# Small products of the recurrent scan in block 1: two steps of the scan issued as one run, on four PSUM banks

## The chip, the cores and the metric

One core of a Trainium2 chip runs the whole program. The metric is device time in microseconds (us), the median of the runs. The engines are PE (TensorE), DVE (VectorE), ACT (ScalarE), POOL (GpSimd) and SP (SyncE, here the queue from which most transfers are issued).

## The reference

The program computes three blocks on 512 tokens of width 1024. The change lies in the first, in its recurrent branch: a gated linear recurrence over chunks of 32 tokens, with 8 heads of 128 x 128 state, run once forward and once backward over the sequence.

```python
HG_CHUNK = 32
def gla_chunk_scan(q, k, v, log_f):            # (B, T, H, 128)
    ...
    qc, kc, vc, gc = chunks(q), chunks(k), chunks(v), chunks(log_f)
    b = jnp.cumsum(gc, axis=3)
    b_last = b[:, :, :, -1, :]
    q_t = qc * jnp.exp(b)
    k_t = kc * jnp.exp(-b)
    k_s = kc * jnp.exp(b_last[:, :, :, None, :] - b)
    a = jnp.where(lower, jnp.einsum('nbhik,nbhjk->nbhij', q_t, k_t), 0.0)
    o_intra = jnp.einsum('nbhij,nbhjv->nbhiv', a, vc)
    def step(state, xs):
        q_n, k_n, v_n, dec_n = xs
        o_n = jnp.einsum('bhik,bhkv->bhiv', q_n, state)
        state = dec_n[..., None] * state + jnp.einsum('bhik,bhiv->bhkv', k_n, v_n)
        return state, o_n
    _, o_inter = lax.scan(step, s0, (q_t, k_s, vc, jnp.exp(b_last)))
    ...
o_fwd = hgrn2_scan(q_b, i_b, zf_fwd, lb_f)
o_bwd = jnp.flip(hgrn2_scan(jnp.flip(q_b, 1), jnp.flip(i_b, 1), jnp.flip(zf_bwd, 1), lb_b), 1)
```

## The kernel before, in words

The recurrent branch is the function `hgrn`. It takes the 8 heads in four pairs. For a pair, `project` makes the projections of the hidden state (queries, the two gates, values, the output gate) with large matrix products; the helper `mm` (L102 to L104) does each as three products of exact halves, so the rows L102, L103 and L104 are the projections. Then `scan` does the recurrence of the pair: `m` counts its two heads, `d` the two directions, and the 16 chunks of 32 tokens are 16 steps.

A step of `scan` has up to eight small products on PE and four vector operations on DVE:

- the o products (L527): queries of the chunk against the state before it. 32 columns of PE are used, and the result goes into 32 partitions of the bank `ob[m]`; `tile_position=(0, po)` says which strip of 32 columns, with po = 32 x (chunk mod 4).
- the u products (L535): keys of the chunk against its values, 32 rows of PE deep, `tile_position=(po, 0)`: a strip of 32 rows. Each step takes two PSUM banks for them, one for each direction, which holds both heads.
- the four operations on DVE (L547, or a copy L544 at the first step): new state = old state x decay + u. The o products of the next step read it.

A product in float32 shows as two instructions in the trace, so a step has 8 + 8 of them.

Order of the work: `scan` and `ends` (normalise, turn and gate the pair's outputs) are generators. While `project` of the next pair runs, a `Side` object advances them by one or two yields at each yield of `project`; what is left when `project` ends is drained (`side.drain()`), and for the last pair the eight gate projections after the loop (L594) do the same. That is the order in which the code is written. A scheduler (the tile framework's, by its own timeline) then orders the instructions of each engine: it takes what is ready by its reckoning, earlier code first. It therefore mixes small products of neighbouring steps, and puts them between projections.

All PSUM tiles of block 1 (`ps`, `o`, `u`) share one ring of eight banks. A scan holds two for `ob`; the projections use one after the other.

## Time and profile before

| | us |
|---|---|
| runs: median (lowest to highest of 3) | 3543.41 (3537.98 to 3550.98) |
| span of the profiled execution | 3547.4 |
| PE busy in it | 3200.2 (90%) |
| DVE busy | 1552.2 (44%) |
| ACT busy | 1013.6 (29%) |
| POOL busy | 971.3 (27%) |

The page gives the profiled execution's span and lists no time around it; the span lies 4.0 us above the median of the runs and inside their range. Busy shares are means over the whole program, whose parts differ. The small products of the scan run from 459 to 859 us of the span, and only that stretch bears on the change.

In a timeline a row is: start, length, engine, line, operation, output and inputs, count. Rows of one PE line that follow one another are merged, and a length includes the time in which a product passes through the array, so the difference of two starts, not the length, is what a product takes from PE.

### The profile page before, as it was taken

To read this page: it belongs to the slowest core of one execution; us is meant where nothing else is said; L and a number is where in the kernel's file an instruction comes from. 1 tells how busy PE (TensorE), PEld (TensorE's weight loads), DVE (VectorE), ACT (ScalarE), POOL (GpSimd) and SP (SyncE) were. 2 spreads that over 40 slices of the span, in tenths; PEclk is the share of its full clock that TensorE was granted. 3 is DMA by queue.
4 is the path that set the end of the run, shared out by engine and by line. 5 is a ranking of instruction groups with operands and counts; after the bars stand their busy time and mean duration, and the time that the engine had idled before them with its cause. 6 is when DMAs were issued, how large, how long until landed. Compare 5 with 4: busy or idle time off the path is not lost.

```text
span 3547.4 us, 52376 instructions
## 1 busy us (share of the span) xinstructions
PE 3200.2 (90%) x21072; PEld 2087.7 (59%) x21072; DVE 1552.2 (44%) x3435; ACT 1013.6 (29%) x2175; POOL 971.3 (27%) x859
## 2 busy tenths in 40 slices
PE   8999999999989889979999999799777578699988
PEld 6898777776766856663333333578656467433322
DVE  3324544423339678542233222531477877422222
ACT  4334323322221356311111111312365452110000
POOL 5343423232332454220000000433564444000000
PEclk9999999999989999879999999899887789899999
DMA  4121211113536433048988886253222133799998
GB/s 152 48 72 53 67 60 59 50 60 93 163 90 181 130 108 102 25 166 341 345 330 335 312 323 260 86 157 121 78 79 63 63 94 115 293 409 409 409 409 350
DMA packets 372551, 625.93 MB, mean 176 GB/s; under 512 B 43998, under 2 KB 240525, under 8 KB 372310
## 3 DMA queue, kind: packets, MB, share of 16 engines
q1 hardware_dynamic: 367190, 603.58, 47.9%
q0 software_dynamic: 5120, 19.01, 1.4%
q8 instruction: 166, 2.72, 0.3%
q14 instruction: 75, 0.61, 0.1%
HBM read 596.61 MB, written 25.91 MB: 175 GB/s over the span
## 4 chain that ended last, share of the span: by engine, by line
PE 73%; DVE 11%; DMA 8%; ACT 4%; issue 2%; POOL 2%; SPq 1%; POOLq 0%; ACTq 0%; DVEq 0%
PE ps L102 11%; PE h L1604 10%; PE ps L103 10%; PE ps L104 10%; PE yb L1643 7%; DMA w<-in_moe_w_dram 5%; PE hc L1604 3%; PE ps L1586 2%; PE o L527 2%; PE u L535 1%; PE ps L913 1%; PE ob L749 1%; DVE acc L1087 1%; PE ps L2240 1%; DMA aw<-in_ada_w_dram 1%
## 5 line engine op out<-in xcount | busy, mean ns | idle before, releaser
L201 POOL TENSOR_TENSOR wlo<-wraw,whi 128x1024 fp32r<-128x1024 f32 (+5 forms) x219 | 422.9, 1952 | 828.6 <-ACT whi L197 810.0
L1604 PE MATMUL h<-w,xT 128*64 128x512 f32 x2048 | 465.1, 601 | 22.4 <-DMA w<-in_moe_w_dram 16.9
L1604 PEld LDWEIGHTS h<-w,xT 128*64 128x64 f32 x2048 | 141.6, 137 | 335.9 <-issue 255.2
L1643 PE MATMUL yb<-w,hT 128*64 128x512 f32 (+1 forms) x1536 | 304.5, 604 | 17.8 <-ACT hT L1627 15.4
L197 ACT CAST whi<-wraw 128x2048 fp32r<-128x2048 f32 (+4 forms) x108 | 161.5, 1496 | 239.2 <-PE ps L103 128.0
L1464 POOL DMA_INDIRECT xs<-xh,ii x20 | 21.3, 1066 | 732.4 <-DVE sl L1467 712.0
L1643 PEld LDWEIGHTS yb<-w,hT 128*64 128x64 f32 (+1 forms) x1536 | 88.0, 129 | 200.6 <-issue 159.2
L1612 DVE SCALAR_TENSOR_TENSOR th<-th,h 128x512 f32<-128x512 f32 x32 | 22.0, 688 | 415.0 <-ACT th L1611 415.0
L102 PE MATMUL ps<-hT,whi 128*128 128x512 f32 x416 | 173.4, 417 | 0.0
L102 PE MATMUL ps<-whi,hT 128*128 128x512 f32 (+1 forms) x424 | 165.2, 390 | 4.0 <-DVE hT L316 4.0
L103 PE MATMUL ps<-hT,wlo 128*128 128x512 f32 x416 | 166.0, 399 | 0.0
L104 PE MATMUL ps<-hT,whi 128*128 128x512 f32 x416 | 165.9, 399 | 0.0
L1611 ACT ACTIVATE th<-h 128x512 f32<-128x512 f32 x32 | 19.1, 597 | 501.5 <-PE h L1604 501.5
L103 PE MATMUL ps<-whi,hT 128*128 128x512 f32 (+1 forms) x424 | 157.4, 371 | 0.0
L104 PE MATMUL ps<-wlo,hT 128*128 128x512 f32 (+1 forms) x424 | 154.5, 367 | 0.0
L115 POOL TENSOR_TENSOR rs<-rs_t,mhalf 128x8 f32<-128x8 f32 (+3 forms) x78 | 95.3, 1226 | 122.3 <-DVE rs_t L110 100.9
L1604 PE MATMUL hc<-w,xT 128*32 128x512 f32 x1024 | 124.2, 598 | 0.0
L1656 DVE TENSOR_TENSOR ys<-yb,g 64x512 f32<-64x512 f32 x64 | 44.1, 689 | 182.8 <-PE yb L1643 182.3
L547 DVE SCALAR_TENSOR_TENSOR s<-s,ec,u 128x128 f32<-128x128 f32 x224 | 65.3, 342 | 128.3 <-PE u L535 126.1
L102 PEld LDWEIGHTS ps<-whi,hT 128*128 128x128 f32 x424 | 104.4, 246 | 15.2 <-issue 4.9
L103 PEld LDWEIGHTS ps<-whi,hT 128*128 128x128 f32 x424 | 104.7, 247 | 7.8 <-issue 3.5
L1087 DVE SCALAR_TENSOR_TENSOR acc<-glu,w,acc 128x798 f32<-128x798 f32 x90 | 107.0, 1223 | 1.0
(810 smaller groups left out, 7031.3 us busy)
## 6 DMA issues: line engine op xcount, KB each, us to landing
w<-in_moe_w_dram SPq DMA_DIRECT2D x376, 1024.0 KB
wraw<-in_w_in_dram SPq DMA_DIRECT2D x48, 1024.0 KB
aw<-in_ada_w_dram SPq DMA_DIRECT2D x192, 256.0 KB
wraw<-in_od_w_in_dram SPq DMA_DIRECT2D x27, 512.0 KB
rows<-rw_rows SPq DMA_DIRECT2D x48, 192.0 KB
w<-in_moe_w_dram POOLq DMA_DIRECT2D x8, 1024.0 KB, 9.1
xh<-xn SPq DMA_DIRECT2D x10, 512.0 KB
wraw<-in_w_proj_b_dram SPq DMA_DIRECT2D x4, 1024.0 KB
```

What stands on the lines that cost most here:

```text
L102: nc.tensor.matmul(out, L[0], R[0], start=start, stop=False)
L103: nc.tensor.matmul(out, L[1], R[0], start=False, stop=False)
L104: nc.tensor.matmul(out, L[0], R[1], start=False, stop=stop)
L115: nc.gpsimd.tensor_tensor(out, t, mh.to_broadcast(list(ss.shape)), op=ALU.pow)
L197: nc.scalar.copy(hi, raw)
L201: eng.tensor_tensor(lo[:, a:b], raw[:, a:b], hi[:, a:b].bitcast(F32), op=ALU.subtract)
L527: nc.tensor.matmul(ob[m][po2:po2 + 32, t2 * 128:t2 * 128 + 128], X["qx", d][:, m, c2], tt[d, m], start=False, stop=(n == 15), skip_group_c ...
L547: nc.vector.scalar_tensor_tensor(s, tt[d, m], X["ec", d][:, m * 16 + cp:m * 16 + cp + 1], u, ALU.mult, ALU.add)
L1087: v.scalar_tensor_tensor(acc[:, c], glu[:, c, j:j + W], w2[:, j, c:c + 1], acc[:, c], ALU.mult, ALU.add)
L1586: nc.tensor.matmul(b, back, y[:, hs], start=(i == 0), stop=(i == len(terms) - 1))
L1604: nc.tensor.matmul(bb[o:o + cap], lhs, w[:, kk % 2, fh * 512:fh * 512 + 512], start=(kk == 0), stop=(kk == 7), tile_position=(0, o))
L1643: nc.tensor.matmul(yb[o:o + cap], lhs, w[:, j, dh * 512:dh * 512 + 512], start=first, stop=last, tile_position=(0, o))
```

## The change

Only `scan` is changed. The loop takes two steps at a time: first the o products of the last two steps, then the u products of the next two, for one head in both directions and both steps, then for the other head. The u products of two steps lie in four banks. Every small product gets an order-only edge (no semaphore) to the last DVE operation of the two steps before it, so the scheduler may not put it ahead of that one. State tiles have three buffers in place of two. There is one yield after each step's vector operations and one after each pair, so a scan now has 24 yields in this loop where it had 16.

```diff
-        tt = {}
-        for n in range(16):
-            if n > 0:
-                for m in range(2):
+        tt, ub, last, st = {}, {}, None, mybir.DependencyInfo(mybir.DependencyClass.NoSync, mybir.DependencyReason.DATA)
+        place = lambda d, n: (n // 4, 32 * (n % 4)) if d == 0 else ((15 - n) // 4, 32 * ((15 - n) % 4))
+
+        def together(mm):
+            if last is not None:
+                k.tc.add_manual_dep(mm.ins, last.ins.name, st, reason="together")
+        for n in range(0, 18, 2):
+            for m in range(2):
+                for i in (n - 2, n - 1):
                     for d in range(2):
-                        c2 = n if d == 0 else 15 - n
...
+                        if i > 0:
+                            c = i if d == 0 else 15 - i
+                            t, po = place(d, i)
+                            together(nc.tensor.matmul(ob[m][po:po + 32, t * 128:t * 128 + 128], X["qx", d][:, m, c], tt[d, m, i - 1],
+                                                      start=False, stop=(i == 15), skip_group_check=True, tile_position=(0, po)))
-            if n < 15:
-                ub = [bank("u"), bank("u")]
+            steps = [i for i in (n, n + 1) if i < 15]
+            for i in steps:
                 for d in range(2):
...
+                    ub[d, i] = bank("u")
+            for m in range(2):
+                for i in steps:
+                    for d in range(2):
+                        t, po = place(d, i)
+                        together(nc.tensor.matmul(ub[d, i][:, m * 128:m * 128 + 128],
+                                                  kt[d][po:po + 32, m, t], v[po:po + 32, t, m * 128:m * 128 + 128],
+                                                  start=True, stop=True, tile_position=(po, 0)))
+            for i in steps:
                 for d in range(2):
...
-                        s = T([128, 128], f"s{d}{m}", 2)
+                        s = T([128, 128], f"s{d}{m}", 3)
...
+                            last = nc.vector.scalar_tensor_tensor(s, tt[d, m, i - 1], X["ec", d][:, m * 16 + cp:m * 16 + cp + 1], u, ALU.mult, ALU.add)
+                        tt[d, m, i] = s
+                yield
             yield
```

What it does to the order of the instructions is seen at three places. In the rows, o is an output bank of a pair, u a bank of u products, s with two digits the state of direction and head, qx the queries, kt the keys, v the values; a number behind a name tells tiles apart.

PE, second pair of heads, one run between projections, as it was before:

```order
L104 MATMUL ps_4158<-hT1_91,whi_3939 128x512
L527 MATMUL o_4018<-s00_4132,qx0_3396 32x128
L535 MATMUL u_4175<-v_3593,kt0_3964 128x128
L527 MATMUL o_4019<-s01_4134,qx0_3396 32x128
L535 MATMUL u_4175<-v_3593,kt0_3964 128x128
L535 MATMUL u_4176<-v_3593,kt1_3992 128x128
L527 MATMUL o_4018<-s10_4136,qx1_3565 32x128
L527 MATMUL o_4019<-s11_4138,qx1_3565 32x128
L527 MATMUL o_4018<-s00_4150,qx0_3396 32x128
L527 MATMUL o_4019<-s01_4152,qx0_3396 32x128
L535 MATMUL u_4176<-v_3593,kt1_3992 128x128
```

PE, the same pair, a run of the changed kernel:

```order
L104 MATMUL ps_4444<-hT1_91,whi_4217 128x512
L536 MATMUL o_4018<-s00_4339,qx0_3380 32x128
L536 MATMUL o_4018<-s10_4343,qx1_3503 32x128
L536 MATMUL o_4018<-s00_4393,qx0_3380 32x128
L536 MATMUL o_4018<-s10_4397,qx1_3503 32x128
L536 MATMUL o_4019<-s01_4341,qx0_3380 32x128
L536 MATMUL o_4019<-s11_4345,qx1_3503 32x128
L536 MATMUL o_4019<-s01_4395,qx0_3380 32x128
L536 MATMUL o_4019<-s11_4399,qx1_3503 32x128
L546 MATMUL u_4465<-v_3541,kt0_3964 128x128
L546 MATMUL u_4466<-v_3541,kt1_3992 128x128
L546 MATMUL u_4467<-v_3541,kt0_3964 128x128
```

Before, o and u products alternate, and neighbours often share a strip; now eight o products stand together, four strips of 32 columns for each head, and then eight u products (five more rows follow) on four strips of 32 rows and four banks. Over the four pairs the small products stood in 80 runs with 142 changes between o and u inside them; now they stand in 31 runs with 33 changes.

PE, second pair, where the projections of the pair have ended and the rest of the scan is drained (new in the changed kernel; the same in the third pair):

```order
L546 MATMUL u_4517<-v_3541,kt0_3964 128x128
L546 MATMUL u_4518<-v_3541,kt1_3992 128x128
L536 MATMUL o_4018<-s00_4485,qx0_3380 32x128
L536 MATMUL o_4018<-s10_4489,qx1_3503 32x128
L536 MATMUL o_4018<-s00_4527,qx0_3380 32x128
L536 MATMUL o_4018<-s10_4531,qx1_3503 32x128
L536 MATMUL o_4019<-s01_4487,qx0_3380 32x128
L536 MATMUL o_4019<-s11_4491,qx1_3503 32x128
L536 MATMUL o_4019<-s01_4529,qx0_3380 32x128
L536 MATMUL o_4019<-s11_4533,qx1_3503 32x128
L546 MATMUL u_4551<-v_3541,kt0_3964 128x128
```

No projection stands between two runs here: three runs, 44 products, follow one another, where before no run had more than 12 products. Elsewhere between two runs of the changed kernel lie 12 to 48 projections.

PE at the end of the branch, before and then in the changed kernel (L568 and L581 turn the outputs of the last pair, oha is the first operand of the next stage):

```order
L103 MATMUL ps_6192<-hT0_90,wlo_6030 128x512
L104 MATMUL ps_6192<-hT1_91,whi_6029 128x512
L568 MATMUL ps_6218<-cc_58,kt0_6169 128x128 x4
L568 MATMUL ps_6225<-cc_58,kt0_6169 128x128 x4
L102 MATMUL ps_6302<-oha0_6237,whi_6147 128x512
```

```order
L546 MATMUL u_6186<-v_4979,kt1_5522 128x128
L536 MATMUL o_5556<-s00_6169,qx0_4822 32x128
L536 MATMUL o_5556<-s10_6173,qx1_4945 32x128
L536 MATMUL o_5557<-s01_6171,qx0_4822 32x128
L536 MATMUL o_5557<-s11_6175,qx1_4945 32x128
L536 MATMUL o_5556<-s00_6191,qx0_4822 32x128
L536 MATMUL o_5557<-s01_6193,qx0_4822 32x128
L536 MATMUL o_5556<-s10_6195,qx1_4945 32x128
L536 MATMUL o_5557<-s11_6197,qx1_4945 32x128
L581 MATMUL ps_6218<-cc_58,kt0_6208 128x128 x4
L581 MATMUL ps_6225<-cc_58,kt0_6208 128x128 x4
L102 MATMUL ps_6302<-oha0_6237,whi_6073 128x512
```

Before, 41 projections lie between the last o product and the first L568; now none. On POOL, the power of the last pair (ors, L115) stood ahead of the two operations of 1024 columns that split the next weights, and now stands behind them:

```order
L201 TENSOR_TENSOR wlo<-wraw,whi 128x512 x2
L201 TENSOR_TENSOR wlo<-wraw,whi 128x1024 x2
L115 TENSOR_TENSOR ors<-rs_t,mhalf 128x8
L201 TENSOR_TENSOR wlo<-wraw,whi 128x512 x2
```

That is the changed kernel; before, the second and third of these rows stood the other way round.

## Rows read from the trace of the kernel before

**Rows 1.** Page, part 1: busy time of each engine.
```profile
PE 3200.2 (90%) x21072; PEld 2087.7 (59%) x21072; DVE 1552.2 (44%) x3435; ACT 1013.6 (29%) x2175; POOL 971.3 (27%) x859
```

**Rows 2.** Windows, 459.2 to 859.2 us: length; busy us of PE, PEld, DVE, ACT, POOL; clock.
```profile
459.20:859.20 400.00, 396.82 (x2372) 301.69 (x2372) 148.62 (x330) 106.05 (x118) 116.14 (x52) 0.99 0.17 55
```

**Rows 3.** Chain of waits, 459 to 860 us, by line (its head).
```profile
by line: PE ps L102 20.0%; PE ps L103 17.9%; PE ps L104 17.7%; PE o L527 13.7%; PE u L535 12.9%; PE ps L511 2.7%; DVE gb L459 2.4%; issue 2.0%; DVE ga L451 1.8%; ACT ga L454 1.3%; PE ps L502 1.3%; DVE gb L457 1.1%; ACT whi L197 0.9%; PE o L
```

**Rows 4.** Groups by form, PE, 459.2 to 859.2 us: busy us, mean ns | idle before.
```profile
L527 PE MATMUL o<-s,qx 128*32 128x128 f32 x480 | 67.1, 283 | 3.2 <-DVE s L547 2.9
L535 PE MATMUL u<-v,kt 32*128 32x128 f32 x480 | 62.4, 305 | 0.0
```

**Rows 5.** Timeline, PE: four u products on two strips; eight on four.
```profile
458.92 0.40 PE L104 MATMUL ps<-hT,whi 128*128 128x512 f32 x1
459.25 0.72 PE L535 MATMUL u<-v,kt 32*128 32x128 f32 x8
459.90 0.50 PE L102 MATMUL ps<-hT,whi 128*128 128x512 f32 x1
...
570.47 0.39 PE L103 MATMUL ps<-hT,wlo 128*128 128x512 f32 x1
570.71 0.40 PE L104 MATMUL ps<-hT,whi 128*128 128x512 f32 x1
571.03 0.75 PE L535 MATMUL u<-v,kt 32*128 32x128 f32 x16
571.71 0.50 PE L102 MATMUL ps<-hT,whi 128*128 128x512 f32 x1
```

**Rows 6.** Timeline, PE: the chopped run shown in the order above.
```profile
574.39 0.40 PE L104 MATMUL ps<-hT,whi 128*128 128x512 f32 x1
574.90 0.41 PE L527 MATMUL o<-s,qx 128*32 128x128 f32 x2
...
578.37 0.50 PE L102 MATMUL ps<-hT,whi 128*128 128x512 f32 x1
```

**Rows 7.** Timeline, PE: four o products on two strips, then eight u products.
```profile
586.79 0.28 PE L103 MATMUL ps<-whi,hT 128*128 128x256 f32 x1
586.91 0.28 PE L104 MATMUL ps<-wlo,hT 128*128 128x256 f32 x1
587.12 0.63 PE L527 MATMUL o<-s,qx 128*32 128x128 f32 x8
587.68 0.75 PE L535 MATMUL u<-v,kt 32*128 32x128 f32 x16
588.35 0.39 PE L102 MATMUL ps<-whi,hT 128*128 128x256 f32 x1
```

**Rows 8.** Timeline, DVE: the state operations of two steps, back to back.
```profile
506.09 2.13 DVE L547 SCALAR_TENSOR_TENSOR s<-s,ec,u 128x128 f32<-128x128 f32 x8
```

**Rows 9.** Timeline, DVE, 587 to 597 us: operations of a direction's gate around states.
```profile
587.72 3.25 DVE L459 TENSOR_TENSOR_SCAN gb<-keep,ga 128x1024 f32<-128x1024 f32 x1 [1.12 <-ACT ga L454]
...
593.43 1.23 DVE L465 TENSOR_TENSOR qt<-q,eb 128x1024 f32<-128x1024 f32 x1 [1.19 <-ACT eb L460]
...
596.49 1.22 DVE L472 TENSOR_TENSOR qx<-qt,ec 128x480 f32<-128x480 f32 x2
```

**Rows 10.** Windows around a wait of PE: columns as in rows 2.
```profile
588.00:593.00 5.00, 3.79 (x37) 2.62 (x30) 4.25 (x6) 1.94 (x2) 0.82 (x1) 1.00 0.60 196
593.00:603.50 10.50, 10.50 (x45) 7.97 (x45) 5.49 (x11) 1.83 (x3) 1.29 (x1) 0.51 0.03 8
```

**Rows 11.** Timeline, all engines, end of the branch: from the last o product on.
```profile
858.65 0.62 PE L527 MATMUL o<-s,qx 128*32 128x128 f32 x4
...
863.38 1.29 DVE L562 TENSOR_TENSOR kt<-o,ors 128x512 f32<-128x512 f32 x2 [1.75 <-POOL ors L115]
...
871.56 5.14 POOL L201 TENSOR_TENSOR wlo<-wraw,whi 128x1024 fp32r<-128x1024 f32 x2 [8.21 <-ACT whi L197]
...
872.03 5.83 DVE L957 TENSOR_TENSOR ola<-oaT,oha 128x512 fp32r<-128x512 f32 x3 [1.08 <-ACT oha L956]
```

More of the change, by code (lines that the diff above doesn't have):

```diff
@@ L519, in scan @@
             yield
-        tt = {}
-        for n in range(16):
-            if n > 0:
-                for m in range(2):
-                    for d in range(2):
-                        c2 = n if d == 0 else 15 - n
-                        t2, po2 = c2 // 4, 32 * (c2 % 4)
-                        nc.tensor.matmul(ob[m][po2:po2 + 32, t2 * 128:t2 * 128 + 128], X["qx", d][:, m, c2], tt[d, m],
-                                         start=False, stop=(n == 15), skip_group_check=True, tile_position=(0, po2))
-            if n < 15:
-                ub = [bank("u"), bank("u")]
-                for d in range(2):
-                    c = n if d == 0 else 15 - n
-                    t, po = c // 4, 32 * (c % 4)
-                    for m in range(2):
-                        nc.tensor.matmul(ub[d][:, m * 128:m * 128 + 128],
-                                         kt[d][po:po + 32, m, t], v[po:po + 32, t, m * 128:m * 128 + 128],
-                                         start=True, stop=True, tile_position=(po, 0))
-                for d in range(2):
-                    c = n if d == 0 else 15 - n
-                    for m in range(2):
-                        u = ub[d][:, m * 128:m * 128 + 128]
-                        s = T([128, 128], f"s{d}{m}", 2)
-                        if n == 0:
-                            nc.vector.tensor_copy(s, u)
@@ new lines, in scan @@
+        tt, ub, last, st = {}, {}, None, mybir.DependencyInfo(mybir.DependencyClass.NoSync, mybir.DependencyReason.DATA)
[6 more added lines that the diff above has]
+                for i in (n - 2, n - 1):
+                    for d in range(2):
+                        if i > 0:
[5 more added lines that the diff above has]
+            for i in steps:
+                for d in range(2):
+                    ub[d, i] = bank("u")
[7 more added lines that the diff above has]
+            for i in steps:
+                for d in range(2):
+                    c = i if d == 0 else 15 - i
+                    for m in range(2):
+                        u = ub[d, i][:, m * 128:m * 128 + 128]
+                        s = T([128, 128], f"s{d}{m}", 3)
+                        if i == 0:
+                            last = nc.vector.tensor_copy(s, u)
```

2 lines of the change are left out of this document (removed).

## The prediction

> **What bounds the kernel now.** I read the page's busy shares first: PE is busy for 90% of the span, DVE for 44% [rows 1]. That is a mean over stages, so I next read the window of the stage that holds the small products: PE is busy for 396.82 of its 400.00 us, DVE for 148.62, ACT for 106.05 and POOL for 116.14, at a granted clock of 0.99 [rows 2]. PE sets the pace there and nothing else is near. The chain of waits says what PE is on it for: projections (L102 to L104) hold over half of the path, and the small products of the scan 13.7% (o) and 12.9% (u) [rows 3], which is 26.6% of 401 us, or 107 us, without the gaps around them. The reader should see that DVE hardly appears there. So time taken from the small products on PE is time taken from the kernel, as long as PE does not begin to wait instead.
>
> How much is there to take? The groups by form give 67.1 us of busy time to the o products and 62.4 to the u products, 129.5 together [rows 4]. A busy time counts the passage through the array that overlaps with what follows: four o products and eight u products with 0.63 + 0.75 = 1.38 busy take 1.32 of PE [rows 7], which is worked out below, 4% less; a run of u products alone takes 0.77 for 0.75 [rows 5]. I take 126 us for all 80 runs, 1.58 for each.
>
> **The change, part by part.**
>
> *What a run costs when it is not chopped.* Projections of 512 columns start 0.24 apart (570.47, 570.71). The projection at 570.71 [rows 5] would have been followed at 570.95; the next starts at 571.71, so eight u products on four strips cost 0.77 us. That is one tenth of a us for each, which shows that strips of 32 rows work at the same time. Projections of 256 columns start 0.12 apart (586.79, 586.91) [rows 7], so the run of four o and eight u products costs 588.35 - 587.03 = 1.32; the o part is 1.32 - 0.77 = 0.55. The chopped run of 12 products costs 578.37 - 574.63 = 3.74 [rows 6], three times as much for as many products: each change between o and u, and each neighbour on the same strip, leaves the array partly idle. Up to here the sum stands on durations that the trace shows.
>
> *The new run of eight o and eight u products.* No run before has eight o products on four strips; the widest has four on two. From below it costs 1.32, if eight on four strips take as long as four on two; from above 1.32 + 0.55 = 1.87, if a second set of four is simply added. The u products show which end is nearer: four of them on two strips cost 0.74 (459.90 - 459.16), eight on four strips 0.77 [rows 5], so the second set of strips is all but free. I take 1.40 because of that, and keep both ends.
>
> The rows show two strips of columns at work together, and no more [rows 7]. The Trainium skill (TensorEngine Tiling (Array Packing), Key Properties) says that tiles operate independently, which with strips of 32 columns means four at once. By that rule a run costs 1.32 and the sum below is 2 us lower; by the upper end it is 12 us higher. No run so far shows four.
>
> *Sum of the runs.* Per pair of heads: one run of eight u (0.77), one of four o and eight u (1.32), five of eight and eight (5 x 1.40 = 7.00), one of eight o and four u (1.37), one of eight o (0.75, between the o part 0.55 and that with a full change of 0.2 on top). That is 11.2, for four pairs 45 us. Gross gain: 126 - 45 = 81 us. At 1.87 the four pairs cost 57.
>
> *Waits that are added.* PE now has places with nothing between a run and the states that the next one reads.
> - Drained runs, in pairs two and three: the extra yields make the scan longer than the projections beside it, so three runs follow one another. Two steps' states take 2.13 us on DVE [rows 8]. The next o products need the first half of it, 1.1, and a start of some 0.2; the next u products need banks that the second half frees, but the o products cover 0.55 of that. I take 1.6 for each place, between 1.1 and 2.4; four places, 6.4 us.
> - End of the branch: the 41 projections that covered the last pair's normalisation are gone, as the order shows. From the last o products at 858.65 to the end of the normalised rows at 863.38 + 1.29 = 864.67 pass 6.0 us [rows 11], of which 0.6 is the products themselves: 5.4 exposed. Before it the state of step 14 is awaited: four operations, 1.1, and a start of 0.2, less 0.4 for the o products that don't need it, 0.9. On POOL the power now stands behind two weight splits that took 5.14 [rows 11]; they can start some 4 us before it, so I leave 1.2 of them ahead of it. On the other side, these splits are then out of the way of what follows them: the next operands (ola) took 5.83 for three on DVE beside POOL's 5.14 [rows 11], and I take 2 back there. Sum 5.4 + 0.9 + 1.2 - 2 = 5.5 us, between 3 and 9.
> - DVE behind a direction's gate: the scan over a gate holds DVE 3.25, then comes a wait for ACT, then qt, kk and qx with about 1.2 each [rows 9]. Before, states were slipped between these; the changed DVE order puts all of them ahead of the next states. From the start of the gate's scan at 587.72 to the end of qx at 597.71 there are 10 us; PE has two stretches of 48 narrow projections (48 x 0.12 = 5.8 each) and a run to cover that. I take 1.5 us for each of three pairs, against 2.9 that PE waits in all now [rows 4]: net 1.6, between 0 and 8.
> - Clock: after the wait near 590 us, where PE was busy for 3.79 of 5.00 us, the granted clock stood at 0.51 for the next 10.5 us [rows 10], the lower of the two levels (1.2 GHz). That cost about 5 us. The drained runs are longer waits than this one. I add 7: five at one more place of the two and two at the end; between 0 and 15.
>
> - Banks: the u products of two steps hold four of eight and the outputs two, so a projection can meet a bank that ACT has not read yet. ACT is idle for 294 of the 400 us [rows 2], so I take 4 us, between 0 and 12.
>
> Together 6.4 + 5.5 + 1.6 + 7 + 4 = 24.5 us. Net: 81 - 24.5 = 56. The number of instructions, transfers and bytes stays, and the order of SP's queue changes at one place far from here. Whatever comes after the branch starts earlier by as much; the scheduler also reorders parts of the attention of the second block, which I cost at nothing, with 8 us either way in the range.
>
> Span 3547.4 - 56 = 3491.4. The span lies 4.0 above the median of the runs, so against the median **3487 us**.
>
> **The rivals.**
>
> *Strips of columns do not work four at once.* The o part doubles: 7 runs with eight o products in each pair, 28 x 0.45 = 13 us more, 3500. For it: nothing in the trace has more than two strips of columns together. Against it: rows and columns of 32 behave alike as far as two go.
>
> *The vector engine becomes the bound of the runs.* Each run makes eight vector operations at once, where before they were spread over two to three runs. If PE waits 1.5 us at every one of the 28 later runs, instead of at a few, that is 42 us in place of the 8 for drained runs and gates, 34 more: 3521; with 2.4 at each, 3546. I put the case at 3530. For it: DVE has 148.62 us of work in the stage, in lumps of up to 3.25 [rows 2, 9]. Against it: 24 projections give 24 x 0.24 = 5.8 us of cover, 2.13 are needed [rows 8]. The Trainium skill (TensorEngine Tiling (Array Packing), PSUM Bottleneck) warns of just this: tiling speeds up TensorE but not the reading of PSUM, which can then become the bottleneck. By that rule this rival would be the forecast; the trace agrees only where no projections stand between two runs.
>
> *Slower: the ring of eight banks runs dry.* Four u banks and two output banks leave two for projections. If the next projection's bank is one that a late state operation still holds, then PE stops in front of the large work, not only the small. DVE can be up to 7.5 us late (3.25 + 1.2 x 3 and its wait) at two gates of a pair, 8 x 7.5 = 60, and 2.4 at the 20 other runs, 48: 108 against 81 gained, 27 slower with the rest at nothing, 3570. It decides from a mean wait of 81/31 = 2.6 us a run. Against it: the run of eight u products today already holds four banks [rows 5], and no wait of that kind shows there.
>
> *The waits do not appear.* If the drained runs find free banks and the clock holds, 8 us of cost are left: 3543 - 73 = 3470.
>
> That the change does not do what it says can be left aside, since the order shows the runs whole.
>
> **How the numbers follow.** Forecast 0.58 (its own range 3465 to 3508), strips 0.14, no waits 0.09, vector engine 0.13, banks 0.06. A measurement of this kernel can tell about 0.5% from no change, 18 us: faster means below 3526. Faster: 0.58 + 0.14 + 0.09 + 0.03 of the vector case = 0.84. Same: 0.10 of the vector case and 0.01 of the banks = 0.11. Slower: 0.05. The range goes from 3462, just below the case without waits, to 3520, above the forecast with both bounds and the strips; half of the vector case, the banks and the forecast's own tails, about 0.2, are left out.
>
> **What would show it.** Right: o and u products together at 45 to 60 us of busy time where they had 129.5; a run of eight and eight at 1.3 to 1.5 us from projection to projection; PE waits on DVE of 1 to 2.4 us at four places in pairs two and three, and one gap of about 5 us before the turning of the last pair (L581); the stretch from the first u to the last o product some 50 to 65 us shorter than 400; a granted clock below 1 behind the drained runs. Wrong: waits of projections (L102) for DVE or ACT inside the scan, a run near 1.9 us, or a gain in the branch that is missing at the end of the program.

## The result, and the profile after

The changed kernel took **3455.34 us** (median of 4 runs, 3452.15 to 3469.11) against 3540.89 for the kernel before, measured beside it (3537.98 to 3550.98, 4 runs): a ratio of 0.9756, with a 95% interval of 0.9729 to 0.9783, or 86 us less. The forecast was 3487 us, with a range from 3462 to 3520. The sign was right, and the gain lies outside the range on the good side. One run of the kernel before among those taken beside the repeats below, 4596.84 us at a granted clock of 0.64, is left out of every median.

The page, part 1, of the changed kernel answers to [rows 1]: as many products, 97 us less of busy PE.

```profile
PE 3103.6 (90%) x21072; PEld 2032.6 (59%) x21072; DVE 1538.3 (45%) x3435; ACT 1013.0 (29%) x2175; POOL 975.3 (28%) x859
```

The window from the first u product to the start of the last o product answers to [rows 2]. It is 331.40 us long, where the same stretch was 399.8 (459.2 to 859.0), and 41 projections more lie in it.

```profile
459.90:791.30 331.40, 326.94 (x2413) 264.33 (x2412) 140.55 (x330) 108.43 (x120) 121.07 (x53) 0.99 0.21 69
```

The groups by form on PE in that window answer to [rows 4]: 129.5 us of small products have become 49.6.

```profile
L536 PE MATMUL o<-s,qx 128*32 128x128 f32 x480 | 25.0, 280 | 0.8
L546 PE MATMUL u<-v,kt 32*128 32x128 f32 x480 | 24.6, 297 | 1.5 <-DVE s L559 1.5
```

The chain of waits over 459 to 792 us answers to [rows 3]. The small products hold 9.8% of it, where they had 26.6%; DVE's states now appear on it with 1.8%.

```profile
by line: PE ps L102 24.3%; PE ps L104 22.9%; PE ps L103 22.9%; PE u L546 5.4%; PE o L536 4.4%; PE ps L511 3.2%; PE o L517 3.2%; issue 2.0%; DVE s L559 1.8%; PE ps L502 1.6%; ACT whi L197 1.1%; DVE ga L451 0.9%; PE ps L581 0.8%; DVE kk L450 
```

*The runs.* The timeline of PE shows a run of four o and eight u products, and then the new one of eight and eight, which no trace had shown:

```profile
466.02 0.39 PE L104 MATMUL ps<-hT,whi 128*128 128x512 f32 x1
466.34 0.63 PE L536 MATMUL o<-s,qx 128*32 128x128 f32 x8
466.90 0.73 PE L546 MATMUL u<-v,kt 32*128 32x128 f32 x16
467.56 0.50 PE L102 MATMUL ps<-hT,whi 128*128 128x512 f32 x1
...
475.86 0.39 PE L104 MATMUL ps<-hT,whi 128*128 128x512 f32 x1
476.18 0.64 PE L536 MATMUL o<-s,qx 128*32 128x128 f32 x16
476.75 0.73 PE L546 MATMUL u<-v,kt 32*128 32x128 f32 x16
477.41 0.51 PE L102 MATMUL ps<-hT,whi 128*128 128x512 f32 x1
```

A projection of 512 columns takes 0.235 from start to start. So the first run costs 467.56 - 466.02 - 0.235 = 1.31 and the second 477.41 - 475.86 - 0.235 = 1.32: the four o products added on two more strips are free. By the same reckoning, from the start of the projection ahead to the start of the one behind, all 31 runs cost 57.0 us with the waits in them; the 80 runs before cost 126.4.

*The waits.* The list of PE's waits from 459 to 801 us has three entries:

```profile
PE ps L581 <- DVE kt L575: 6.8, 1, 6.8
PE ps L102 <- ACT v L481: 2.2, 1, 2.2
PE u L546 <- DVE s L559: 1.5, 1, 1.5
```

The drained runs of pair two, in PE's timeline; the waits hide in the length of the merged rows (1.69 and 1.67 for o products that take 0.65 elsewhere):

```profile
593.03 0.65 PE L536 MATMUL o<-s,qx 128*32 128x128 f32 x16
...
594.26 1.69 PE L536 MATMUL o<-s,qx 128*32 128x128 f32 x16
...
596.53 1.67 PE L536 MATMUL o<-s,qx 128*32 128x128 f32 x16
...
598.78 0.50 PE L102 MATMUL ps<-hT,whi 128*128 128x512 f32 x1
```

The group costs 5.84; its three runs alone would be 3.95 (1.32, 1.32 and 1.31). That is 1.9 of wait here and the same in pair three, 3.8 together. The clock did not fall on it. In windows over the drained runs and over the 10 us behind them (columns as in rows 2) the granted clock is 1.00, the upper of the two levels, where [rows 10] had 0.51:

```profile
593.00:599.00 6.00, 5.60 (x90) 3.35 (x90) 5.04 (x18) 2.38 (x2) 3.40 (x2) 1.00 0.00 0
599.00:609.00 10.00, 10.00 (x56) 7.72 (x56) 3.11 (x8) 1.67 (x3) 2.93 (x2) 1.00 0.34 107
```

*The end of the branch* answers to [rows 11]: normalising now runs uncovered, with POOL's power (L115) behind two weight splits, as the order had it.

```profile
791.23 4.66 POOL L201 TENSOR_TENSOR wlo<-wraw,whi 128x1024 fp32r<-128x1024 f32 x2 [12.41 <-ACT whi L197]
...
796.00 1.63 POOL L115 TENSOR_TENSOR ors<-rs_t,mhalf 128x8 f32<-128x8 f32 x1
797.66 1.29 DVE L575 TENSOR_TENSOR kt<-o,ors 128x512 f32<-128x512 f32 x2 [1.75 <-POOL ors L115]
798.41 1.97 PE L581 MATMUL ps<-cc,kt 128*128 128x128 f32 x8 [6.84 <-DVE kt L575]
```

**Where the time went.** I cut each trace at five marks, each the start of an instruction: the first u product, the last o product, the last turn (L568, now L581), the first cast of the operands of the second block's attention (16 in a row, L956, now L969), and the last of the experts' first products (L1604, now L1617). All figures are in us; the last line is the time that the trace's record of the granted clock shows at the lower level (1.2 GHz) between the fourth mark and the fifth.

```
                                    before    after
first u to last o                    399.8    331.4
last o to last turn                   10.7      8.7
last turn to first cast              151.8    147.3
  together                           562.3    487.4    -75
first cast to last expert product   2501.2   2478.3    -23
  of that at the lower clock           396      352
```

So 75 us come from the branch, its end and the stage behind it, and 23 from code that the change does not touch, though the scheduler orders some of it otherwise. Together that is more than the 86 us between the medians, because the two profiled executions lie 97 us apart (3547.4 and 3450.3): that of the changed kernel is its fastest run, at a mean granted clock of 0.945, and that of the kernel before stands at 0.938. The experiments had to explain both parts.

### The profile page after: what moved, and what is told of

Its sections match the earlier page's. It is cut to its first block, busy times and chain, and to the rows that moved or that the text cites. A ratio compares the mean times of both kernels' runs of the same rounds, so it can differ in the third digit from the quotient of the medians.

```text
span 3450.3 us, 52389 instructions
## 1 busy us (share of the span) xinstructions
PE 3103.6 (90%) x21072; PEld 2032.6 (59%) x21072; DVE 1538.3 (45%) x3435; ACT 1013.0 (29%) x2175; POOL 975.3 (28%) x859
## 4 chain that ended last, share of the span: by engine, by line
PE 73%; DVE 11%; DMA 8%; ACT 4%; issue 2%; POOL 2%; SPq 1%; POOLq 0%; DVEq 0%; ACTq 0%
PE ps L102 11%; PE h L1617 10%; PE ps L103 10%; PE ps L104 10%; PE yb L1656 7%; DMA w<-in_moe_w_dram 6%; PE hc L1617 4%; PE ps L1599 2%; PE ps L926 1%; PE ob L762 1%; PE ps L2253 1%; DVE acc L1100 1%; DVE pr L2308 1%; DVE N L2309 1%; PE ob L1303 1%
## 5 line engine op out<-in xcount | busy, mean ns | idle before, releaser
L1617 PE MATMUL h<-w,xT 128*64 128x512 f32 x2048 | 462.6, 597 | 23.7 <-DMA w<-in_moe_w_dram 18.1
L1617 PEld LDWEIGHTS h<-w,xT 128*64 128x64 f32 x2048 | 141.1, 137 | 335.0 <-issue 253.9
L115 POOL TENSOR_TENSOR rs<-rs_t,mhalf 128x8 f32<-128x8 f32 (+3 forms) x78 | 94.7, 1218 | 113.5 <-DVE rs_t L110 93.7
L1617 PE MATMUL hc<-w,xT 128*32 128x512 f32 x1024 | 124.2, 598 | 0.0
L104 PEld LDWEIGHTS ps<-wlo,hT 128*128 128x128 f32 x424 | 103.9, 246 | 5.2 <-issue 0.2
```

What stands on the lines that cost most here:

```text
L104: nc.tensor.matmul(out, L[0], R[1], start=False, stop=stop)
L115: nc.gpsimd.tensor_tensor(out, t, mh.to_broadcast(list(ss.shape)), op=ALU.pow)
L1617: nc.tensor.matmul(bb[o:o + cap], lhs, w[:, kk % 2, fh * 512:fh * 512 + 512], start=(kk == 0), stop=(kk == 7), tile_position=(0, o))
```

## The experiments

Most expectations on the whole time turned out to mix these two. I therefore compare the stretch from the first u product to the first cast, 487.4 us in the changed kernel and called **the stretch** below, and the cost of the runs in it.

**The changed kernel again, and three edits of it, on one chip.** No edit:

> The changed kernel again, beside the others of this call. Both theories: 3455 us within 8, some 85 below the kernel before. Theory A (two parts): of the 85, about 70 to 75 lie in block 1 (runs whole, four strips at once, few waits) and 8 to 10 in the attention of the second block, whose instructions the scheduler put in another order. Theory B (one part): all of the gain is in block 1, and what the two profiles differ by behind it comes from one execution to the next; then the stretch from the end of block 1 to the first expert product differs between executions of one kernel by as much as between the two kernels, about 10.

Measured: 3466.75 us (3453.86 to 3469.31, 4 runs) against 3537.11 for seven runs of the kernel before, 70 us less in place of 86; the ratio is 0.979 (0.9758 to 0.9823) and the stretch 486.6. The 3455 within 8 that both theories expected was missed, and this second median lies inside the range of the forecast. The eight runs of the changed kernel on the two chips lie in two groups: four at 3452 to 3457 us with a mean granted clock of 0.943 to 0.945, and four at 3464 to 3469 with 0.938 to 0.939. Both profiled executions belong to the first group; the stretch is the same in both.

*Neighbours on the same strip.* The products of a run in another sequence: the two heads of a step, which use the same strip, next to one another.

```diff
-            for m in range(2):
-                for i in (n - 2, n - 1):
-                    for d in range(2):
+            for i in (n - 2, n - 1):
+                for d in range(2):
+                    for m in range(2):
```

(and the same for the u products)

> Runs, edges and banks of the changed kernel, but the two heads of a step next to each other, so that neighbours share a strip. If four strips at once are what makes a run cheap, a run of eight and eight costs 2.2 to 2.6 us in place of 1.32, 25 to 35 us more over all runs; if fewer changes between o and u alone do it, it stays near 1.35. Its order behind block 1 is that of the kernel before but for a few rows: theory A adds 8 to 10 us there against the changed kernel, theory B nothing. Time: 3490 to 3500 with strips and A, 3480 to 3490 with strips and B, 3465 with changes alone and A, 3455 with changes alone and B.

Measured: 3478.53 us, ratio 0.9818 (0.9785 to 0.9851); the stretch 494.3. The run is the one at 476.18 above, in PE's timeline:

```profile
475.94 0.39 PE L104 MATMUL ps<-hT,whi 128*128 128x512 f32 x1
476.26 0.66 PE L536 MATMUL o<-s,qx 128*32 128x128 f32 x16
476.86 0.75 PE L546 MATMUL u<-v,kt 32*128 32x128 f32 x16
477.53 0.51 PE L102 MATMUL ps<-hT,whi 128*128 128x512 f32 x1
```

It costs 1.35, as was expected if fewer changes between o and u do the work; the 2.2 to 2.6 for neighbours that hold each other up did not come. So the sequence inside a group is nearly free. This says nothing against strips at work together, since the fullest strip holds as many products in both sequences. A reading that fits, though no trace shows it directly, is that a product that waits for its own strip does not hold up the next one on another strip. The 7 us that the stretch is longer are for the most part not the sequence, which at 0.03 to 0.04 a run makes about 1 us: projections wait for ACT for 7.8 us in three places, against 2.2 in one, and 10 us of the branch pass at the lower clock, against 3.4.

*One step at a time.* The edges stay, the loop takes single steps again (15 yields).

```diff
-        for n in range(0, 18, 2):
+        for n in range(0, 17, 1):
-                for i in (n - 2, n - 1):
+                for i in (n - 1,):
-            steps = [i for i in (n, n + 1) if i < 15]
+            steps = [i for i in (n,) if i < 15]
-            yield
```

> Edges kept, but one step for each run: four o and four u products on two strips each, two banks. A run then costs 1.30 as in the trace before (four o and four u products, two strips), twice as many runs: about 80 us for all in place of 57 with its waits. If the pairing of two steps matters: 3475 to 3485. If the edges alone, which keep a run whole, brought the gain: within 5 us of the changed kernel.

Measured: 3499.68 us (3494.14 to 3500.82), ratio 0.9878 (0.9844 to 0.9911); the stretch 512.3. The runs cost 77.3 us, near the 80 expected, but the whole lies 15 us above the expected 3475 to 3485. Where two steps follow one another, PE's timeline shows four groups:

```profile
470.06 0.39 PE L104 MATMUL ps<-hT,whi 128*128 128x512 f32 x1
470.38 0.63 PE L536 MATMUL o<-s,qx 128*32 128x128 f32 x8
470.94 0.71 PE L546 MATMUL u<-v,kt 32*128 32x128 f32 x8
471.59 0.63 PE L536 MATMUL o<-s,qx 128*32 128x128 f32 x8
472.15 0.71 PE L546 MATMUL u<-v,kt 32*128 32x128 f32 x8
472.79 0.51 PE L102 MATMUL ps<-hT,whi 128*128 128x512 f32 x1
```

The same sixteen products cost 2.50 in four groups and 1.32 in two; a group of four on two strips takes as long as one of eight on four. With single steps some 48 of the 73 us of the stretch are thus there, and the pairing of steps gives the rest. The 48 are not the edges alone: the sequence by heads, the third buffer of the states and the number of yields also differ from the kernel before, and no run takes these apart.

*No yield after a pair* (15 yields, so nothing is drained):

```diff
                 yield
-            yield
```

> The changed kernel without the yield after each pair of steps: a scan has 15 yields in its loop in place of 24, so nothing is left to drain at the end of a pair, and projections cover the end of the branch. If the waits at drained runs (2.1 us at each of two pairs) and before the last turning (6.8) cost what the profile of the changed kernel shows: 3445 to 3449, 6 to 10 us less. If shorter covers between the runs (down to 4 projections) bring as many waits on DVE elsewhere: within 3 us of the changed kernel.

Measured: 3459.93 us (3444.49 to 3466.43), ratio 0.9764 (0.972 to 0.9808), not to be told from the changed kernel. The runs cost 49.5 us in place of 57.0 and the branch to the last o product is 12 us shorter, of which some 9 are 40 projections that now come behind it. Yet the stretch is 483.8, only 3 to 4 us shorter: the last turn and the stage behind it take 8 us more. The list of PE's waits behind the last turn has two that the changed kernel lacks, for the operands of the next products:

```profile
PE ps L104 <- DVE ola L969: 2.7, 2, 1.5
...
PE ps L102 <- ACT oha L968: 2.1, 1, 2.1
```

and POOL's timeline has the weight split that stood at 791.23 above no earlier:

```profile
791.74 5.14 POOL L201 TENSOR_TENSOR wlo<-wraw,whi 128x1024 fp32r<-128x1024 f32 x2 [7.88 <-ACT whi L197]
```

So the 6.8 us that PE waits at the end of the changed kernel are mostly not lost: ACT, DVE and POOL have work then for which PE would wait next. Added up over the stretch, the waits of PE are 17.7 us in the changed kernel and 16.3 here.

**Does the wait lower the clock?** One yield for each pair of steps (9 yields), so that the scan runs faster than the projections can cover it:

```diff
-                yield
             yield
```

> The changed kernel with one yield for each pair of steps and none after each step: 9 yields in the loop. Runs and edges are kept; covers between runs fall to 0 to 4 projections at several places, but nothing is left to drain. The order behind block 1 is nearly that of the kernel before. Theory A: 583 to 590 us from the splits to the first expert product. Theory C: 576. The branch from the first u to the last o product: 335 to 350 us if the uncovered waits, about 2 us each, count; the last o product comes earlier, under other projections, and if waits do not count 320.

Measured: 3498.41 us in one run; the stretch is 514.2, 27 us longer. The branch is 330.8, neither the 335 to 350 nor the 320 expected, but it is no like measure: it holds 1064 projections where the changed kernel has 1188, and the others come behind the last o product. The o products inside one run, in PE's timeline, then windows over it and behind it:

```profile
580.95 0.41 PE L536 MATMUL o<-s,qx 128*32 128x128 f32 x4
586.24 1.58 PE L536 MATMUL o<-s,qx 128*32 128x128 f32 x12 [4.88 <-DVE s L559]
```
```profile
579.00:590.00 11.00, 5.31 (x72) 3.47 (x71) 8.26 (x16) 4.59 (x5) 6.66 (x3) 0.69 0.29 98
590.00:604.00 14.00, 14.00 (x146) 12.72 (x147) 5.61 (x22) 1.69 (x3) 0.00 (x0) 0.87 0.00 1
```

PE is busy for 5.31 of 11 us and the granted clock is 0.69 there and 0.87 behind; in the branch 30.7 us pass at the lower level, against 3.4 in the changed kernel, and PE waits 22 us for DVE. What DVE does in the 4.88 us, in its timeline:

```profile
579.95 2.29 DVE L459 TENSOR_TENSOR_SCAN gb<-keep,ga 128x1024 f32<-128x1024 f32 x1 [0.28 <-ACT ga L454]
584.70 1.23 DVE L465 TENSOR_TENSOR qt<-q,eb 128x1024 f32<-128x1024 f32 x1 [2.46 <-ACT eb L460]
585.84 1.12 DVE L559 SCALAR_TENSOR_TENSOR s<-s,ec,u 128x128 f32<-128x128 f32 x4
```

The states stand behind a gate's scan, a wait of DVE for ACT and a multiplication of the gate. So the long waits, 3.5 to 4.9 us, come from the order on DVE that the prediction priced under "DVE behind a direction's gate", and they appear as soon as the cover goes. The Trainium skill (TensorEngine Tiling (Array Packing), PSUM Bottleneck) says that tiling speeds up TensorE but not the reading of PSUM. This run does not bear that out: in this wait the states, which read PSUM, take 1.12 us, and the gate and ACT the rest.

**The price of a group.** If a change between o and u costs, four groups of which each is one product deep on its strip must tell it from the price of the products. The o and u products of one head, then those of the other:

```diff
         for n in range(0, 18, 2):
+            steps = [i for i in (n, n + 1) if i < 15]
+            for i in steps:
+                for d in range(2):
+                    ub[d, i] = bank("u")
             for m in range(2):
                 for i in (n - 2, n - 1):
...
-            steps = [i for i in (n, n + 1) if i < 15]
-            for i in steps:
-                for d in range(2):
-                    ub[d, i] = bank("u")
-            for m in range(2):
                 for i in steps:
```

> The changed kernel with o and u products of one head, then o and u of the other: four groups in a run in place of two, each one product deep on a strip in place of two; nothing else. If a group costs 0.2 us for the change and 0.21 for each product on the fullest strip: 1.7 to 1.8 us a run, branch 10 to 14 us longer than 331. If a group costs a fixed 0.6 whatever it holds: 2.5 a run, branch 30 to 35 us longer.

Measured: 3471.82 us in one run; the stretch 493.9. In PE's timeline (the second half of the run is left out):

```profile
475.93 0.40 PE L104 MATMUL ps<-hT,whi 128*128 128x512 f32 x1
476.26 0.42 PE L540 MATMUL o<-s,qx 128*32 128x128 f32 x8
476.62 0.50 PE L545 MATMUL u<-v,kt 32*128 32x128 f32 x8
...
477.84 0.50 PE L102 MATMUL ps<-hT,whi 128*128 128x512 f32 x1
```

The run costs 477.84 - 475.93 - 0.235 = 1.67, within 0.03 of the 1.7 that the model gave; a flat price of 0.62 a group would be 2.5. So a run costs about 0.2 us for each group and 0.21 for each product on its fullest strip, to within some 0.1 us a run: the model gives 1.24, 1.64 and 2.48 where 1.32, 1.67 and 2.50 were measured. The Trainium skill (TensorEngine Tiling (Array Packing), Key Properties) says that a change of the tiling mode drains TensorE; the runs fit that with those 0.2 us for each group, though no trace shows a drain by itself. The branch is 7 us longer, less than the 10 to 14 expected: its runs cost 67.4 us, 10 more, but the 2.2 us wait for ACT is absent.

**Without the edges.** Two steps at a time, four banks and the yields stay:

```diff
-            if last is not None:
+            if False:
```

> The changed kernel without the order-only edges; two steps at a time, four banks, three state tiles and 24 yields stay. By the order, projections and most runs stand as in the changed kernel, and the small products are chopped again only where nothing covers them: 38 runs with 56 changes inside, 94 groups in place of 64. Theory (the gain of the branch is the number of groups, 0.2 us each, and 0.21 for each product on the fullest strip): 30 groups more, branch 5 to 9 us longer than the 331 of the changed kernel, the whole 3460 to 3468. Rival (the edges also keep products from standing in front of projections while they wait): waits of PE on the states inside projections, branch 345 or more, the whole above 3475. If the edges cost instead (they delay what is ready): branch below 331.

Measured: 3476.59 us (3471.3 to 3479.92), ratio 0.9814 (0.9785 to 0.9842); the stretch 500.6, the runs 69.2 in place of 57.0. The branch is 13 us longer, where 5 to 9 were expected, and the whole lies where the rival put it. The list of PE's waits is that of the changed kernel again (6.1 for the last pair, 2.2 and 1.5), so the rival's mechanism is absent; the theory's is there, but 30 groups more cost 12 us. Half of that lies in the drained runs of pairs two and three, which are now chopped into 15 groups in place of 6 (8.8 us each in place of 5.84). For the rest PE's timeline shows why, in what was a run of eight o products behind the drained ones (nine products here):

```profile
603.56 0.84 PE L536 MATMUL o<-s,qx 128*32 128x128 f32 x8
...
604.76 0.41 PE L536 MATMUL o<-s,qx 128*32 128x128 f32 x2
...
606.70 0.62 PE L536 MATMUL o<-s,qx 128*32 128x128 f32 x4
...
608.38 0.62 PE L536 MATMUL o<-s,qx 128*32 128x128 f32 x4
```

Those pieces among projections cost 0.97, 0.52, 0.64 and 0.64, in all 2.8, where the whole run costs 0.67: a piece is a group of its own, so it pays the 0.2 and a depth of its own. Of the 73 us of the stretch, the edges are worth some 14 where the steps are paired.

**The 23 us behind.** First the kernel before once more, and delayed: 60 clearings of the first tile of x on DVE ahead of its load, which overwrites them.

> The kernel before, profiled once more. Theory A (order): its stretches up to the first expert product repeat: 400 us from the first u to the last o product, 152 from the last turning to the splits of the second block, 586 from there to the first expert product, each within 1 us. Theory B (execution to execution): the last differs by 5 to 10 us.

> The kernel before with 60 clearings of the first input tile ahead of its load (their results are overwritten by the load), so that everything starts some 35 to 60 us later. The recurrent branch is that of the kernel before, but the scheduler, which sees the later start, orders the second block's attention much as it does in the changed kernel. Theory A: 400 us for the branch, and 576 (within 4) from the splits to the first expert product, as in the changed kernel. Theory C (the attention is shorter because of what block 1 does): 400 and 586.

```diff
+            for _ in range(60 if t == 0 else 0):
+                nc.vector.memset(x, 0.0)
             nc.sync.dma_start(x, I["x"][0, t * 128:(t + 1) * 128])
```

Measured, one run each: 3551.15 and 3605.23 us. The second block's attention (first cast to the first expert product) took 591.5 and 586.2 us, against 586.2 in the profile of before and 575.9 in the changed kernel's. Two expectations failed: the stages do not repeat within 1 us, and the order of instructions behind block 1, which in the delayed kernel is nearly that of the changed one, does not bring an attention of 576. All that lies behind the first cast is shorter there, though, 2491.7 us against 2501.2 and 2506.0.

Then the changed kernel with the same delay, and both with half of it (30 clearings):

> The changed kernel with 60 clearings of the first tile of x on DVE before its load, which only delays the program by some 67 us (the loaded tile overwrites them). The attention of the second block ran at the lower clock for 102 us in both profiles of the changed kernel, and for 117, 128 and 130 in three of the kernel before (the third delayed in this way). Theory A (the granted clock there goes with the exact order and timing of one kernel, and the change happened on a good one): the half-clock time moves away from 102, to 110 to 130, and the attention takes 580 to 590 in place of 576. Theory B (it belongs to what the change does to the stage): 98 to 106 again, 574 to 578. The branch stays at 331 with 4 either way by both. One look, so 3517 to 3540 by both.

> The kernel before with 30 clearings of the first tile of x on DVE ahead of its load (overwritten by it): the whole program some 33 us later. It is to be compared with the changed kernel delayed in the same way, over several runs. With 60 clearings the two stood 64 us apart (one look each), the branch, the turn and the merge 73 and the rest 9 the other way, where the undelayed kernels stand 86 apart. Theory A (what the change itself gives is the 70 to 75 us of the branch and its end; the rest of the 86 is the granted clock behind it, which goes with the exact timing): half-clock time of the attention 110 to 135 here. 3560 to 3580.

> The changed kernel with the same 30 clearings. Theory A: branch 331, turn 8.7, merge 147, so 70 to 75 less than the kernel before so delayed, and the attention and what follows between 15 less and 10 more by the clock: 60 to 90 us apart. Theory B (the attention is faster because of the change): the attention 574 to 578 here and at least 10 below the delayed kernel before, 82 to 90 us apart, and the run with 60 clearings was the odd one.

Measured: 3541.07 us in one run with 60 clearings; with 30, 3571.13 us (3569.14 to 3584.66, 5 runs) for the kernel before and 3509.57 (3502.26 to 3511.39, 4 runs) for the changed one: 62 us apart, 64 with 60 clearings. The mean granted clock of the profiled executions is 0.938 before and 0.945 after without a delay, and 0.943 and 0.940 with 30 clearings. Cut by the marks:

```
                                       no delay             30 clearings    60 clearings
                            before again  after  r_after   before  after   before  after
the stretch                  562.3 558.7  487.4   486.6     559.9  483.9    559.9  486.5
attention                    586.2 591.5  575.9   576.4     585.4  593.8    586.2  586.9
behind the first cast       2501.2 2506.0 2478.3 2481.8    2494.1 2508.0   2491.7 2501.9
  at the lower clock           396   403    352    348       376    396      379    393
  less half of that           2303  2305   2302   2308      2306   2310     2302   2306
order of the attention           b     b      a      a         n      b        a      b
```

The line "less half of that" is an estimate of what the code behind the first cast would take at the upper level. It is the same for all eight within 8 us, and 2302 to 2309 in the other six profiles, so what differs behind the first cast follows the time at the lower clock. The stretch gains 72 to 76 us at each delay; the attention's 576 is gone in both delayed runs of the changed kernel; and what comes behind gives 23 us or takes back 10 to 14. That is theory A of the delayed runs, in which the 23 us go with the exact order and timing of the kernel; three of its figures come out just outside (76 us for 70 to 75, 14 for 10, and 3541 us for 3540).

Order and timing are not the same thing, and the traces tell them apart better than the delay does. The last line compares ACT's instructions from the first cast to the first expert product: b is the order of the kernel before, a that of the changed kernel (both within 6 of some 520 instructions; a and b differ in 27), n neither. The delay moved the order too: both delayed runs of the changed kernel have the order of the kernel before, and that of the kernel before with 60 clearings has the changed kernel's. Over all 14 profiles, the five of order a (with those of one yield fewer after a pair and of no edges) take 2478 to 2492 us behind the first cast, the seven of order b (with those of neighbours on the same strip, of single steps and of one yield for each pair) 2498 to 2508, and the two of order n 2492 and 2494. In the attention alone the undelayed profiles part in the same way, 576 to 585 us with order a and 586 to 595 with order b, much as the first expectation above gave 8 to 10 us to the order. So the share behind goes with the order that the scheduler gives to the second block, which the edit changes on its way. No run changed that order alone, and what in it lowers the clock stays open. It is not all of the spread either: at one order and one start, the runs of the changed kernel differ by 17 us.

## Why the prediction was wrong, point by point

**What bounds the kernel: right.** Time taken from the small products on PE came off the stretch, less waits that can be listed. PE waits 3.7 us in the branch and 6.8 at its end.

**The runs: right, at the lower bound.** 1.40 was taken and 1.32 measured; 45 us for the 31 runs became 42.5 (0.75, 1.30, five times 1.32, 1.30 and 0.67 in each pair). The lower end that the prediction named was the exact figure. Of its two reasons for the cost of a chopped run, the change between o and u holds, with 0.2 us for a group, whichever strips it uses; the neighbours on the same strip do not (1.35 against 1.32).

**The waits and the clock: the step that failed in the branch.** 24.5 us were put against the gain, which was too much. To the last turn, with the 2 us taken back left for the stage behind (the 126.4 of the runs before hold 2.9 of waits):

```
                           forecast   measured
80 runs less 31              -81       -81   (126 - 45; 123.5 - 42.5)
drained runs                   6.4       3.8 (5.84 - 3.95, twice)
end of the branch              7.5       7.9 (9.83 of the last run, less its products)
DVE behind gates, net          1.6       0   (2.9 now, 2.9 before)
banks                          4         2.2 (a projection for ACT, once)
clock                          7         2   (4 us at the lower level at the end)
sum                          -54.5     -65
stage behind                  -2        -4 to -9
```

The marks themselves give -67 to the last turn (339.3 in the second profile of the changed kernel, 406.0 in the second of the kernel before, neither with time at the lower clock ahead of the last o product), and -70 in the first two profiles, where the kernel before spent 10 us of the branch at the lower clock. So a few us are not accounted for. The places were right, and the clock is the largest error: 7 us were put for it and 2 found. The 4 to 9 us of the stage behind fit the mechanism that was given for 2: two waits of PE for its operands, 2.7 and 2.1 us in the kernel before, are gone. I took the 5 us behind the wait in [rows 10] for what such a wait costs, and the drained runs for longer waits. They are about 1.0 us each, two in a pair, and the clock stayed up behind them. The price itself was one execution's: in the second profile of the kernel before, which has the same wait (1.22 us there, 1.21 in the first), the two windows of [rows 10] read

```profile
588.00:593.00 5.00, 3.78 (x40) 2.73 (x37) 4.53 (x6) 1.88 (x4) 1.38 (x1) 1.00 0.50 163
593.00:603.50 10.50, 10.50 (x73) 7.77 (x73) 6.11 (x14) 2.76 (x4) 1.29 (x1) 1.00 0.07 24
```

The same wait, and no dip; nor is there one in the branch of the two delayed profiles of the kernel before.

**"Whatever comes after starts earlier by as much": the second step that failed, and the larger surprise.** The prediction saw that the scheduler reorders the attention, and put nothing on it, with 8 us either way. In the profiles it is 23 us, by the granted clock: 396 us at the lower level behind the first cast, and 352 after the change. About 10 of the 23 lie in the attention and 13 behind it. In the medians less of it is left: 86 us on the first chip, 11 more than the stretch gives, and 70 on the second, some 4 less. With a delay, where the changed kernel has the order of the kernel before, 10 to 14 us go the other way, and 62 and 64 are measured. So the stretch alone brings the time to the lower end of the range (3541 less 75 is 3466), and what took the first median below 3462 came from this term, with some luck in the executions: the same start less 70, 64 or 62 us lies inside.

**The rivals.** Strips that do not work four at once are refuted by 1.32. DVE as the bound, and the ring of banks that runs dry, do not show in the changed kernel (one wait of 1.5 us for DVE in the branch, and one of 2.2 for ACT, whose copy empties a bank). One yield for each pair of steps brings waits for DVE about, but by the gates and not by the reading of PSUM. The prediction's remark that the trace before agrees with that rival where no projections stand between two runs does not hold: its longest wait,

```profile
591.26 0.41 PE L527 MATMUL o<-s,qx 128*32 128x128 f32 x2 [1.21 <-DVE s L547]
```

has twelve narrow projections ahead of it, and DVE was held by a gate's scan (587.72 in [rows 9]). "The waits do not appear" (3470) was nearest, and its 73 us are what the stretch gained, but by luck: waits of some 14 us did appear where it left 8, and the stage behind, with its 4 to 9 us, made up for them.

## What to carry to other kernels

Count the groups, not the products: with strips of 32 each uninterrupted group of one kind costs some 0.2 us and then the depth of its fullest strip, so gather what fits on all strips, and pin it together, because a scheduler that does not know that price will chop it. Keep large products between the groups, enough to cover the vector work of a group and what else stands ahead of it on the vector engine: the long waits here came from a gate's operations in DVE's order, and the short uncovered ones of the drained runs cost only themselves. An edit can change the order that a scheduler gives to code far behind it, and in a kernel that runs at two clock levels that moves the time: compare the order there, and the time stage by stage, before the whole difference is given to the edit.

## What was not expected of the hardware

- The sequence in which the products of a group are issued hardly matters: neighbours on the same strip cost 1.35 a run against 1.32.
- Four products of one group on two strips, and eight on four, cost the same 0.56 to 0.57 us (start of the o products to start of the u products, 466.34 to 466.90 and 476.18 to 476.75).
- The same wait of 1.2 us was followed by 10.5 us at the lower clock in one execution of the kernel before and by none in another.
- The same code behind the first cast took 2478 to 2508 us in 14 profiles, by the time at the lower clock, and the profiles part by the order of the attention's instructions: 2478 to 2492 for the changed kernel's order, 2498 to 2508 for that of the kernel before.
